# One order for the last four normalisations across three engines, and four gathered rows moved from ahead of the expert loop into it

## The chip, the core and the metric

The kernel runs on one core of a Trainium2 chip. The metric is device microseconds of one execution; the time before is the median of three runs, 1522.99 us (1522.4 to 1523.95). The core's engines are TensorE (PE, matmuls; PEld is its weight load), VectorE (DVE), ScalarE (ACT), GpSimd (POOL) and SyncE (SP, which here issues transfers). Line numbers are those of the kernel before.

## What is computed

One encoder layer on 512 tokens of width 1024: layer norm, a projection, neighbourhood and latent attention, layer norm, then the part that matters here, a feed-forward of 16384 experts (`peer_ffn`), a gated extra term, and a last layer norm:

```python
idx = (e1 * PEER_N_KEYS + e2).reshape(PEER_CHUNK, PEER_HEADS * PEER_TOPK)
g = jax.nn.softmax(cv, axis=-1).reshape(PEER_CHUNK, -1)
u = u_table[idx]
hpre = jnp.einsum('td,ted->te', xb, u)
act = g * jax.nn.gelu(hpre, approximate=False)
return jnp.einsum('te,ted->td', act, v_table[idx])
...
h = layer_norm(DN_ALPHA * h + ffn + ple, ln2_g[i], ln2_b[i])
```

Each token picks 128 experts (8 heads of 16). An expert is one row of U (1024 numbers) and one of V. `layer_norm` subtracts the mean of a token's 1024 values, divides by the root of the variance plus 1e-5, multiplies by `ln2_g` and adds `ln2_b`.

## The kernel before

Tokens lie in four row blocks of 128 partitions, numbered 0 to 3. Block 0 (`c < NGC`) goes the sparse way: for each of its 128 picks k, GpSimd issues an indirect transfer that gathers one U row per token into a `gat` tile (128 x 1024, 512 KB in all; eight such buffers), and DVE multiplies it by the tokens and sums (`gather_u`, L1264, or `rows`, L964, for the first 31). After a Gelu, 128 V rows are gathered in the same way and added, weighted, into `base[0]` (`gather_v`, L1273). Together these are 257 steps (`gather_steps`, L1279).

Blocks 1 to 3 (384 tokens) go the dense way: `lead_block` (L1031) and `expert_in` multiply them by all 128 blocks of U, and the loop at L1340 multiplies the gated result by all 128 blocks of V, in a chosen `order`. Per loop step n it loads one V block (512 KB, `load_v`), splits it into a high and a low part (`split`, L106: ScalarE rounds, DVE subtracts), every second step scales and splits a G tile, and does 18 matmuls of 512 columns into six PSUM accumulators `acc[c][hf]`, two halves for each of the three blocks. The last four steps are held back in `late` and done accumulator by accumulator (L1388), so that `acc` of block 1 is ready first and that of block 3 last.

The gather steps are dealt out along this loop. `room(n)` (L1329) gives each step a weight; after step n, as many gather steps have been issued as the share of weights used up so far (L1384). `PRE` says how many U rows were done ahead of the loop: 31 in an earlier stage (`BESIDE`), `SOME` = 4 whose transfers are issued first in the block at L1307, ahead of the two loads of the first G tile on GpSimd's queue, and six more (`PRE` - `BESIDE` - `SOME`) behind those loads. By this arithmetic 27 gather steps fall to n = 112 to 124. The order on DVE and SP is the program's (`manual_schedule`); in the block at L1307 also that of ScalarE, TensorE and GpSimd.

The end (L1394 to L1406) has no such order: for each block, the two halves of `acc` are added into `base[c]` with a running sum (blocks 1 to 3, L1402), then `layer_norm` (L135). Block 0 takes mean and variance by batch-norm statistics on DVE (L142); the others take the mean from the sums and the variance from a Square on ScalarE (L152). Then a root on ScalarE (L155), a refinement by four 128x1 operations on DVE (`rsqrt_refine`, L128), two 128x1024 operations on DVE (L162 or L164, L165), and one transfer out per block. The four chains are interleaved by the scheduler. GpSimd has no part in it.

Of the kernel before, what the change touches and what calls it, by code (L numbers as in the profile page):

```python
# [9 lines left out]
F32 = mybir.dt.float32  # L10
# [4 lines left out]
AF = mybir.ActivationFunctionType  # L15
OP = mybir.AluOpType
# [3 lines left out]
D = 1024  # L20
# [7 lines left out]
EPS = 1e-5  # L28
# [8 lines left out]
WIDE = 40  # L37
LEAD = 104
# [3 lines left out]
PACE = 1.07  # L42
AHEAD = 14.0
LAG = 6.0
PRE = 41
SOME = 4
EARLY = 15
EARLY_AT = 4
BESIDE = 31
# [12 lines left out]
GATS = 8  # L62
NO_GATHER = 1
GE_AHEAD = 12
CLOSE = 31
# [13 lines left out]
def tile_encoder_layer(ctx: ExitStack, tc: tile.TileContext, A: dict, out: bass.AP):  # L79
    nc = tc.nc  # L80
# [3 lines left out]
    small = ctx.enter_context(tc.tile_pool(name="small", bufs=4))  # L84
# [11 lines left out]
    w_top = keep.tile([128, 2], F32, name="w_top")  # L96
# [533 lines left out]
    for hf in range(2):  # L630
        hs = slice(hf * 512, (hf + 1) * 512)
# [13 lines left out]
    NGC, NDC = N_G // 128, N_D // 128  # L645
# [607 lines left out]
    pG = ctx.enter_context(tc.tile_pool(name="pG", bufs=1, reuse_waits="tile"))  # L1253
    pP = ctx.enter_context(tc.tile_pool(name="pP", bufs=2, reuse_waits="tile"))
    psA = ctx.enter_context(tc.tile_pool(name="psA", bufs=1, space=PSUM, reuse_waits="tile"))
    acc = [[psA.tile([128, 512], F32, name=f"acc{c}{hf}") for hf in range(2)] for c in range(NDC)]
# [16 lines left out]
    def gather_v(c, k):  # L1273
        u = pG.tile([128, D], F32, name="gat", bufs=GATS)
        nc.gpsimd.indirect_dma_start(out=u[:], out_offset=None, in_=v_rows,  # L1275
                                     in_offset=bass.IndirectOffsetOnAxis(ap=i_sel[:, c, k:k + 1], axis=0))
        nc.vector.scalar_tensor_tensor(base[c], u, hdot[:, c, k:k + 1], base[c], op0=OP.mult, op1=OP.add)  # L1277

    def gather_steps():  # L1279
        for c in range(NGC):  # L1280
# [19 lines left out]
    def blocks_ahead(n):  # L1300
        for _ in range(8 * n):
            next(pe_work, None)

    steps = list(gather_steps())
    late = []

    with tc.manual_schedule(engines={nc.vector.engine, nc.scalar.engine, nc.tensor.engine, nc.sync.engine,  # L1307
                                     nc.gpsimd.engine}):
# [13 lines left out]
        for n in range(2):  # L1322
            v_cut[n] = cut_v(n)
            blocks_ahead(1)
        for k in range(BESIDE + SOME, PRE):
            gather_u(0, k)
        for _ in pe_work:
            pass
    def room(n):  # L1329
        if n < NO_GATHER or n > 124:  # L1330
            return 0.0
        return 2.2 if n + LEAD < 126 else 1.6 if n < CLOSE else 1.0 if n < WIDE else 1.42 if n < 112 else 1.9

    rooms = sum(room(n) for n in range(128))
    done, spent = PRE, 0
    with tc.manual_schedule(engines={nc.vector.engine, nc.sync.engine}):
# [56 lines left out]

    lg = row_bcast(pG, A["ln2_g"], "gat", GATS)  # L1394
    lb = row_bcast(pG, A["ln2_b"], "gat", GATS)
    for c in range(4):
        fsum = None
        if c >= NGC:
            fsum = small.tile([128, 2], F32, name="fsum", bufs=2)
            for hf in range(2):  # L1400
                hs = slice(hf * 512, (hf + 1) * 512)
                nc.vector.scalar_tensor_tensor(base[c][:, hs], acc[c - NGC][hf], w_top[:, 0:1] if c == NGC else 1.0,  # L1402
                                               base[c][:, hs], op0=OP.mult, op1=OP.add,
                                               accum_out=fsum[:, hf:hf + 1])
        layer_norm(base[c], lg, lb, fsum, None if fsum is None else pG.tile([128, D], F32, name="gat", bufs=GATS))
        nc.sync.dma_start(out[c * 128:(c + 1) * 128, :], base[c])  # L1406


# [85 lines left out]
```

## Time and profile before

| | |
|---|---|
| median of three runs | 1522.99 us |
| the profiled execution | 1525.05 us |
| its span, first to last instruction | 1523.2 us |
| busy PE / DVE / ACT / POOL | 95% / 83% / 36% / 41% |
| mean granted TensorE clock | 0.99 |
| moved by DMA | 456.15 MB, mean 299 GB/s |
| first matmul of the V loop | 915.1 us from the span's start |
| last subtraction of the loop on DVE ends | about 1501.9 us |
| last matmul begins | 1511.1 us |

Times in a row are microseconds from the span's start and the duration. Behind `x` stands the number of instructions merged into a row; in square brackets, how long the engine sat idle before it and what ended that. `a<-b,c` names the tile written and the tiles read. "issue" is time in which the engine waited for nothing that the profile shows.

### The profile page before, as it was taken

What the parts mean: (1) busy time and instruction counts of PE and PEld (TensorE: products, weight loads), DVE (VectorE), ACT (ScalarE), POOL (GpSimd) and SP (SyncE); (2) the same over time, 40 slices, a digit from 0 to 9 for tenths busy, and PEclk for the clock granted to TensorE, in tenths of its full rate; (3) what the DMA queues carried; (4) which work ended last, traced back from release to release, by engine and by line L of the source; (5) the groups of instructions that cost most, each with busy time, mean ns of one, the idle gap of its engine ahead of it and who ended that gap; (6) DMA issues with size and microseconds to landing.
All of it is one profiled execution on the core that took longest, in us unless ns stands there. A gap on an engine that the chain in (4) does not pass through costs nothing.

```text
span 1523.2 us, 21811 instructions
## 1 busy us (share of the span) xinstructions
PE 1451.8 (95%) x7715; PEld 1221.4 (80%) x7715; DVE 1267.5 (83%) x2638; ACT 544.4 (36%) x893; POOL 627.7 (41%) x537
## 2 busy tenths in 40 slices
PE   6999999999999999898989989999999999999996
PEld 4788777788888888687877868898788888888875
DVE  7376795668999999899779938988789999989998
ACT  3265685333311232222322323444333333333333
POOL 1013110043355644253235345655545555556560
PEclk9999999999999999899999999999999999999999
DMA  7233241194389999899879999999999999999992
GB/s 238 66 115 92 86 125 43 49 300 147 105 291 322 394 416 413 301 396 398 314 258 409 412 388 392 391 392 335 341 389 396 402 398 398 402 396 400 394 362 113
DMA packets 188414, 456.15 MB, mean 299 GB/s; under 512 B 16400, under 2 KB 80272, under 8 KB 185232
## 3 DMA queue, kind: packets, MB, share of 16 engines
q1 hardware_dynamic: 121264, 211.45, 38.8%
q0 software_dynamic: 58400, 208.69, 36.3%
q10 hardware_dynamic: 8640, 34.61, 5.6%
q8 instruction: 61, 1.00, 0.3%
q14 instruction: 49, 0.40, 0.1%
HBM read 413.01 MB, written 38.80 MB: 297 GB/s over the span
## 4 chain that ended last, share of the span: by engine, by line
PE 42%; DVE 20%; issue 15%; DMA 14%; POOL 6%; ACT 2%; SPq 1%; POOLq 0%; DVEq 0%; ACTq 0%
DMA raw<-in_v_rows_dram 7%; PE acc L126 5%; PE acc L124 5%; PE acc L125 5%; PE pj L124 3%; PE pj L125 3%; PE pj L126 3%; DMA raw<-in_uT_dram 3%; DVE base L1277 3%; PE mm L1042 3%; POOL row L968 2%; PE mm L124 2%; PE mm L126 2%; POOL wlo L968 2%; PE mm L125 2%
## 5 line engine op out<-in xcount | busy, mean ns | idle before, releaser
L1275 POOL DMA_INDIRECT gat<-in_v_rows_dram,i_sel x128 | 192.8, 1506 | 140.8 <-DVE base L1277 119.5
L1042 PE MATMUL hp<-whole,raw 128*128 128x256 f32 x816 | 193.4, 393 | 21.1 <-DMA raw<-in_uT_dram 21.1
L1260 POOL DMA_INDIRECT gat<-in_u_rows_dram,i_sel x97 | 149.4, 1541 | 121.8 <-DVE gat L1266 93.6
L1042 PEld LDWEIGHTS hp<-whole,raw 128*128 128x128 f32 x816 | 158.9, 197 | 45.6 <-issue 13.2
L126 PE MATMUL acc<-v_hi,a_lo 128*128 128x512 f32 x456 | 178.4, 392 | 2.6 <-DVE a_lo L110 2.5
L124 PE MATMUL acc<-v_hi,a_hi 128*128 128x512 f32 x456 | 178.3, 391 | 1.5 <-ACT v_hi L109 1.1
L125 PE MATMUL acc<-v_lo,a_hi 128*128 128x512 f32 x456 | 177.8, 390 | 0.8 <-DVE v_lo L110 0.8
L109 ACT CAST whi<-raw 128x1024 fp32r<-128x1024 f32 (+4 forms) x103 | 102.7, 997 | 198.7 <-DMA raw<-in_v_rows_dram 101.4
L1277 DVE SCALAR_TENSOR_TENSOR base<-gat,hdot,base 128x1024 f32<-128x1024 f32 x128 | 165.0, 1289 | 1.8
L110 DVE TENSOR_TENSOR wlo<-raw,whi 128x1024 fp32r<-128x1024 f32 (+4 forms) x103 | 118.6, 1152 | 42.7 <-ACT whi L109 41.8
L109 ACT CAST v_hi<-v_raw 128x1024 fp32r<-128x1024 f32 x76 | 79.9, 1052 | 144.7 <-DMA v_raw<-in_v_rows_dram 66.0
L1042 PE MATMUL mm<-whole,raw 128*128 128x256 f32 x560 | 126.7, 382 | 4.4 <-DMA raw<-in_uT_dram 4.4
L126 PE MATMUL acc<-whi,a_lo 128*128 128x512 f32 x312 | 121.6, 390 | 0.3 <-DVE a_lo L110 0.3
L125 PE MATMUL acc<-wlo,a_hi 128*128 128x512 f32 x312 | 121.5, 390 | 0.2 <-DVE wlo L110 0.2
L110 DVE TENSOR_TENSOR v_lo<-v_raw,v_hi 128x1024 fp32r<-128x1024 f32 x76 | 92.6, 1218 | 34.4 <-ACT v_hi L109 34.1
L124 PE MATMUL acc<-whi,a_hi 128*128 128x512 f32 x312 | 120.9, 389 | 0.0
L1266 DVE SCALAR_TENSOR_TENSOR gat<-gat,h 128x1024 f32<-128x1024 f32 x97 | 115.0, 1219 | 6.7 <-DMA gat<-in_u_rows_dram,i_sel 6.7
L1042 PEld LDWEIGHTS mm<-whole,raw 128*128 128x128 f32 x560 | 104.4, 190 | 18.8 <-DMA raw<-in_uT_dram 3.8
L126 PEld LDWEIGHTS acc<-v_hi,a_lo 128*128 128x128 f32 x456 | 85.6, 188 | 23.6 <-DVE a_lo L110 6.2
L124 PEld LDWEIGHTS acc<-v_hi,a_hi 128*128 128x128 f32 x456 | 85.6, 188 | 20.3 <-ACT a_hi L109 1.7
L125 PEld LDWEIGHTS acc<-v_lo,a_hi 128*128 128x128 f32 x456 | 85.7, 188 | 18.1 <-DVE v_lo L110 1.1
L1023 ACT ACTIVATE ge_ring<-hp 128x256 f32<-128x256 f32 x85 | 32.4, 381 | 146.0 <-PE hp L1042 123.9
(395 smaller groups left out, 3382.7 us busy)
## 6 DMA issues: line engine op xcount, KB each, us to landing
raw<-in_uT_dram SPq DMA_DIRECT2D x110, 512.0 KB
v_raw<-in_v_rows_dram SPq DMA_DIRECT2D x78, 512.0 KB
raw<-in_v_rows_dram SPq DMA_DIRECT2D x50, 512.0 KB
g_dram<-g_st ACTq DMA_DIRECT2D x24, 1024.0 KB
ge_dram<-ge_ring ACTq DMA_DIRECT2D x36, 256.0 KB
g_wide<-g_dram SPq DMA_DIRECT2D x9, 1024.0 KB
raw<-in_w_in_dram SPq DMA_DIRECT2D x17, 512.0 KB
raw<-in_w_q_dram SPq DMA_DIRECT2D x16, 512.0 KB
```

Source lines behind the costliest of these rows:

```text
L109: nc.scalar.copy(hi, src)
L110: nc.vector.tensor_tensor(lo, src, r32(hi), op=OP.subtract)
L124: nc.tensor.matmul(ps, a[0], b[0], start=start, stop=False)
L125: nc.tensor.matmul(ps, a[0], b[1], start=False, stop=False)
L126: nc.tensor.matmul(ps, a[1], b[0], start=False, stop=stop)
L968: nc.gpsimd.indirect_dma_start(out=u[:np], out_offset=None, in_=u_rows, in_offset=bass.IndirectOffsetOnAxis(ap=ix[:np, k:k + 1], axis=0))
L1023: nc.scalar.activation(ge_t[i - i % 2][:, i % 2], ps[:, :N_U], AF.Gelu)
L1042: nc.tensor.matmul(ps[:, :N_U], raw[k], whole[:, k, :], start=(k == 0), stop=(k == 7))
L1260: nc.gpsimd.indirect_dma_start(out=u[:], out_offset=None, in_=u_rows, in_offset=bass.IndirectOffsetOnAxis(ap=i_sel[:, c, k:k + 1], axis=0))
L1266: nc.vector.scalar_tensor_tensor(u, u, 1.0, h[c], op0=OP.mult, op1=OP.mult, accum_out=hdot[:, c, k:k + 1])
L1275: nc.gpsimd.indirect_dma_start(out=u[:], out_offset=None, in_=v_rows, in_offset=bass.IndirectOffsetOnAxis(ap=i_sel[:, c, k:k + 1], axis=0))
L1277: nc.vector.scalar_tensor_tensor(base[c], u, hdot[:, c, k:k + 1], base[c], op0=OP.mult, op1=OP.add)
```

## The change

Two things change. First, `PRE` goes from 41 to 37 and `SOME` from 4 to 0: the four early rows are no longer gathered ahead of the G loads; six rows (31 to 36) stay behind them, and the loop deals out 220 steps instead of 216. The weight of n = 112 to 124 goes from 1.9 to 2.1, by which 30 steps fall there.

Second, the end is written out by hand on DVE, ScalarE, GpSimd and SP. The sum for block 0's mean comes from the last `gather_v` (`accum_out`), in place of the batch-norm statistics, and its variance from a Square on ScalarE like the others'. Blocks 0 and 2 finish "aside": ScalarE applies scale and offset (Identity), GpSimd multiplies by `ln2_g` and adds `ln2_b`, and one transfer goes out. Blocks 1 and 3 finish on DVE: one operation `centre`, then two halves with a transfer each.

```diff
-PRE = 41
-SOME = 4
+PRE = 37
+SOME = 0
...
-        nc.vector.scalar_tensor_tensor(base[c], u, hdot[:, c, k:k + 1], base[c], op0=OP.mult, op1=OP.add)
+        nc.vector.scalar_tensor_tensor(base[c], u, hdot[:, c, k:k + 1], base[c], op0=OP.mult, op1=OP.add,
+                                       **({"accum_out": fsum[c][:, 0:1]} if k == 127 else {}))
...
-        return 2.2 if n + LEAD < 126 else 1.6 if n < CLOSE else 1.0 if n < WIDE else 1.42 if n < 112 else 1.9
+        return 2.2 if n + LEAD < 126 else 1.6 if n < CLOSE else 1.0 if n < WIDE else 1.42 if n < 112 else 2.1
...
+    def take(c, hf):
+        hs = halves[hf]
+        nc.vector.scalar_tensor_tensor(base[c][:, hs], acc[c - NGC][hf], w_top[:, 0:1] if c == NGC else 1.0,
+                                       base[c][:, hs], op0=OP.mult, op1=OP.add, accum_out=fsum[c][:, hf:hf + 1])
+
+    def mean(c):
+        if c < NGC:
+            nc.vector.tensor_scalar(neg[c], fsum[c][:, 0:1], -1.0 / D, None, op0=OP.mult)
+        else:
+            nc.vector.tensor_tensor(neg[c], fsum[c][:, 0:1], fsum[c][:, 1:2], op=OP.add)
+            nc.vector.tensor_scalar(neg[c], neg[c], -1.0 / D, None, op0=OP.mult)
+        nc.scalar.activation(pG.tile([128, D], F32, name="gat", bufs=GATS), base[c], AF.Square, bias=neg[c],
+                             accum_out=ve[c])
+
+    def root(c):
+        nc.vector.tensor_scalar(ve[c], ve[c], 1.0 / D, EPS, op0=OP.mult, op1=OP.add)
+        nc.scalar.sqrt(sd[c], ve[c])
+
+    def refine(c):
+        nc.vector.reciprocal(sd[c], sd[c])
+        rsqrt_refine(inv[c], sd[c], ve[c], off[c])
+
+    def aside(c):
+        nc.vector.tensor_tensor(off[c], neg[c], inv[c], op=OP.mult)
+        nc.scalar.activation(base[c], base[c], AF.Identity, bias=off[c], scale=inv[c])
+        nc.gpsimd.tensor_tensor(base[c], base[c], lg, op=OP.mult)
+        nc.gpsimd.tensor_tensor(base[c], base[c], lb, op=OP.add)
         nc.sync.dma_start(out[c * 128:(c + 1) * 128, :], base[c])
+
+    def centre(c):
+        x = pG.tile([128, D], F32, name="gat", bufs=GATS)
+        nc.vector.scalar_tensor_tensor(x, base[c], neg[c], lg, op0=OP.add, op1=OP.mult)
+        return x
+
+    def finish(c, x, hf):
+        hs = halves[hf]
+        nc.vector.scalar_tensor_tensor(x[:, hs], x[:, hs], inv[c], lb[:, hs], op0=OP.mult, op1=OP.add)
+        nc.sync.dma_start(out[c * 128:(c + 1) * 128, hs], x[:, hs])
```

The order, each line on the engines that it names above: mean(0); take(1, 0), take(1, 1), mean(1); root(0); take(2, 0); refine(0), aside(0); one = centre(1); root(1); take(2, 1), mean(2); refine(1), finish(1, one, 0), finish(1, one, 1); root(2); take(3, 0); refine(2), aside(2); take(3, 1), mean(3); three = centre(3); root(3), refine(3); finish(3, three, 0), finish(3, three, 1).

More of the change, by code (lines that the diff above doesn't have):

```diff
@@ L1305, in tile_encoder_layer @@
     late = []
+    fsum = [small.tile([128, 2], F32, name=n, bufs=4 if n == "ln_mu" else 2)
+            for n in ("ln_mu", "fsum", "fsum", "ln_mu")]
     with tc.manual_schedule(engines={nc.vector.engine, nc.scalar.engine, nc.tensor.engine, nc.sync.engine,
@@ L1395, in tile_encoder_layer @@
     lb = row_bcast(pG, A["ln2_b"], "gat", GATS)
[L1396 to L1405, printed above, removed]
-        nc.sync.dma_start(out[c * 128:(c + 1) * 128, :], base[c])
+    neg = [small.tile([128, 1], F32, name="ln_y0") for c in range(4)]
@@ new lines, in tile_encoder_layer @@
+    ve = [small.tile([128, 1], F32, name="ln_ve") for c in range(4)]
+    sd = [small.tile([128, 1], F32, name="ln_sd") for c in range(4)]
+    inv = [small.tile([128, 1], F32, name="ln_y") for c in range(4)]
+    off = [small.tile([128, 1], F32, name="ln_t") for c in range(4)]
+    halves = [slice(0, 512), slice(512, 1024)]
+    def take(c, hf):
+        hs = halves[hf]
+        nc.vector.scalar_tensor_tensor(base[c][:, hs], acc[c - NGC][hf], w_top[:, 0:1] if c == NGC else 1.0,
+                                       base[c][:, hs], op0=OP.mult, op1=OP.add, accum_out=fsum[c][:, hf:hf + 1])
@@ new lines, in finish @@
+    def finish(c, x, hf):
+        hs = halves[hf]
+        nc.vector.scalar_tensor_tensor(x[:, hs], x[:, hs], inv[c], lb[:, hs], op0=OP.mult, op1=OP.add)
+        nc.sync.dma_start(out[c * 128:(c + 1) * 128, hs], x[:, hs])
+    with tc.manual_schedule(engines={nc.vector.engine, nc.scalar.engine, nc.gpsimd.engine, nc.sync.engine}):
+        mean(0)
+        take(1, 0)
+        take(1, 1)
+        mean(1)
+        root(0)
+        take(2, 0)
+        refine(0)
+        aside(0)
+        one = centre(1)
+        root(1)
+        take(2, 1)
+        mean(2)
+        refine(1)
+        finish(1, one, 0)
+        finish(1, one, 1)
+        root(2)
+        take(3, 0)
+        refine(2)
+        aside(2)
+        take(3, 1)
+        mean(3)
+        three = centre(3)
+        root(3)
+        refine(3)
+        finish(3, three, 0)
+        finish(3, three, 1)
```

## The prediction

> **What bounds the kernel now.** The profiled execution spans 1523.2 us and took 1525.05 us, so 1.85 us lie around the span; the median of the runs is 1522.99 us. I make the sum against the span and add it to the median. A measurement of this kernel can tell about 0.2% (3 us) from no change.
>
> I read the page first, then a table by stage around the two edited places (the columns are the window, its length, busy us and count of PE, PEld, DVE, ACT and POOL, the granted clock, the DMA share and GB/s).
>
> ```profile
> PE 1451.8 (95%) x7715; PEld 1221.4 (80%) x7715; DVE 1267.5 (83%) x2638; ACT 544.4 (36%) x893; POOL 627.7 (41%) x537
> ```
>
> ```profile
> 880.00:892.00 12.00, 5.07 (x23) 3.80 (x21) 5.12 (x10) 0.77 (x2) 1.89 (x3) 0.97 1.02 368
> 892.00:896.00 4.00, 3.43 (x8) 2.81 (x9) 0.00 (x0) 0.00 (x0) 3.08 (x4) 0.50 1.03 374
> 896.00:900.00 4.00, 4.00 (x15) 3.28 (x15) 0.00 (x0) 0.38 (x1) 3.09 (x4) 0.72 1.02 367
> ...
> 1100.00:1440.00 340.00, 339.36 (x1495) 280.13 (x1494) 309.13 (x316) 119.23 (x125) 190.48 (x125) 1.00 1.04 397
> 1440.00:1492.00 52.00, 50.49 (x218) 40.08 (x217) 51.54 (x48) 15.68 (x17) 28.27 (x19) 1.00 0.92 353
> ```
>
> The whole says PE; the stages say three different things. From 1100 to 1440 PE is the limit (busy 339.36 of 340.00) while DVE has 31 us to spare: a gather row added there is hidden. From 1440 to 1492, the blocks 112 to 123, DVE has half a microsecond left in 52: a row added there is paid. From 880 to 900, just ahead of the loop, PE is busy 5.07 of 12 us and the DMA share is above 1: DMA is the limit. After 1502 come the four normalisations, where the wait that ends last must be followed op by op.
>
> **The opening: four rows fewer.** Timelines of PE, POOL, DVE and ACT, and the DMA total from 865 to 905.5:
>
> ```profile
> 882.40 3.72 PE L1042 MATMUL hp<-whole,raw 128*128 128x256 f32 x16 [1.06 <-DMA raw<-in_uT_dram]
> 892.57 6.49 PE L1042 MATMUL hp<-whole,raw 128*128 128x256 f32 x16 [6.44 <-DMA raw<-in_uT_dram]
> 898.90 7.07 PE L1042 MATMUL hp<-whole,whi 128*128 128x256 f32 x32
> ```
>
> ```profile
> 865.08 1.43 POOL L1260 DMA_INDIRECT gat<-in_u_rows_dram,i_sel  x1 [0.30 <-issue]
> ...
> 878.53 0.94 POOL L1260 DMA_INDIRECT gat<-in_u_rows_dram,i_sel  x1 [0.30 <-DMA raw<-in_uT_dram]
> ```
>
> ```profile
> 890.56 1.23 DVE L1266 SCALAR_TENSOR_TENSOR gat<-gat,h 128x1024 f32<-128x1024 f32 x1 [1.34 <-DMA gat<-in_u_rows_dram,i_sel]
> ...
> 904.36 1.23 DVE L110 TENSOR_TENSOR v_lo<-v_raw,v_hi 128x1024 fp32r<-128x1024 f32 x1 [12.56 <-ACT v_hi L109]
> ```
>
> ```profile
> 905.47 1.04 ACT L109 CAST whi<-raw 128x1024 fp32r<-128x1024 f32 x1 [1.14 <-DMA raw<-in_uT_dram]
> ```
>
> ```profile
> DMA packets 3921, 15.87 MB, mean 392 GB/s; under 512 B 416, under 2 KB 416, under 8 KB 3555
> ```
>
> The four SOME rows go out on POOL from 865.08 to 878.53, ahead of both loads of the first G tile; DVE consumes the last one at 890.56 and then sits idle for 12.56 us. So their DVE work (4 x 1.23 us) is hidden and its removal worth nothing, and so is the POOL time; the cover is that idle stretch. What they cost is traffic: 4 x 128 rows x 4 KB = 2.10 MB, at 392 GB/s 5.35 us, in a stretch where PE waits 6.44 us for a U block and ScalarE waits for the next (905.47). With PRE at 37 the same six rows (31 to 36 instead of 35 to 40) stay behind the G loads, and eight gat buffers cap what is drawn forward, so the bytes are really gone from this stage. The first G load moves ahead on POOL's queue from behind 878.53 to 865 at the earliest; its bytes were due in this stage anyway. Bounds: nothing, if the queues re-divide the time and the U block still lands last; and PE's whole stall, 6.44 us of idle plus the slow matmuls behind it: at 0.22 us each (7.07 us for 32) 34 would fit between 892.57 and 900, and at the clock of 0.50 and 0.72 there were 23, so 2.4 us more, together 8.8. I take the bytes, 5.35, because ScalarE's wait for DMA at 905.47 caps what PE could win alone.
>
> Of the four rows one returns in blocks 0 to 111 (the count that `room` gives falls from 4 behind to 3 there) and three in blocks 112 to 124 (27 before, 30 after: 1.9 becomes 2.1). The first is hidden under PE unless DMA, at 397 GB/s beside it, is as tight as PE, when it costs 0.52 MB / 392 GB/s = 1.35; I take half. Gain up to block 112: 5.35 - 0.65 = 4.7 us.
>
> **The tail: three rows more.** From the chain of waits, two pairs of rows between their neighbours, and the group of blocks 112 to 123:
>
> ```profile
> 1440.41 1.21 DVE base L1277
> ...
> 1442.84 0.15 DVE wlo L110
> ...
> 1443.98 1.33 DVE base L1277
> ...
> 1446.69 0.44 issue
> ```
>
> ```profile
> L1277 DVE SCALAR_TENSOR_TENSOR base<-gat,hdot,base 128x1024 f32<-128x1024 f32 x25 | 32.3, 1291 | 0.5
> ```
>
> Two rows take 2.43 us and two take 2.71, so 1.29 each, as the group's mean. DVE is full here, and everything behind stands in its order: 3 x 1.29 = +3.9 us. It could be as little as 2.5 if DVE enters block 112 further ahead.
>
> **The end.** Before, the last subtraction of the loop ends at 1501.9 and the span ends 21.3 us later. Rows of DVE, ACT and SP:
>
> ```profile
> 1500.78 1.22 DVE L110 TENSOR_TENSOR v_lo<-v_raw,v_hi 128x1024 fp32r<-128x1024 f32 x1
> ...
> 1503.11 0.74 DVE L1402 SCALAR_TENSOR_TENSOR h<-acc,w_top,h 128x512 f32<-128x512 f32 x1
> ...
> 1517.71 0.16 DVE L131 TENSOR_TENSOR ln_t<-ln_t,ln_y 128x1 f32<-128x1 f32 x1
> 1517.91 0.15 DVE L132 TENSOR_SCALAR ln_t<-ln_t 128x1 f32<-128x1 f32 x1
> ...
> 1518.29 1.28 DVE L165 SCALAR_TENSOR_TENSOR h<-h,ln_y,gat 128x1024 f32<-128x1024 f32 x1
> ```
>
> ```profile
> 1499.80 1.28 ACT L155 ACT_TABLE_LOAD   x1
> ...
> 1506.70 1.15 ACT L152 ACTIVATE gat<-h,ln_mu 128x1024 f32<-128x1024 f32 x1 [1.80 <-DVE ln_mu L149]
> ```
>
> The earlier normalisation has ScalarE's order Square, then root, as the new end has:
>
> ```profile
> 278.80 1.15 ACT L152 ACTIVATE raw<-h,ln_mu 128x1024 f32<-128x1024 f32 x1 [5.90 <-DVE ln_mu L149]
> ...
> 280.06 1.28 ACT L155 ACT_TABLE_LOAD   x1
> 281.35 0.20 ACT L155 ACTIVATE ln_sd<-ln_ve 128x1 f32<-128x1 f32 x1
> ```
>
> There the table load comes only behind the Square. Now it is hidden at 1499.80, because the root is first; afterwards it stands behind two Squares and ahead of root 0, on the path. The Trainium skill, in "ScalarE: Activation LUTs", section What ACT_TABLE_LOAD costs, gives about 2.66 us for a switch, load and drain; here the root follows 1.29 us after the load's start, so I go by the row, and by the page the end would be 1.4 us later (1531.6).
>
> GpSimd gets four operations, multiply and add for row blocks 0 and 2. What it does to DVE is shown where GpSimd computes earlier (POOL rows, DVE rows, POOL's group):
>
> ```profile
> 369.50 2.47 POOL L852 TENSOR_TENSOR wlo<-raw,whi 128x1024 fp32r<-128x1024 f32 x1 [4.10 <-ACT whi L851]
> 382.88 2.58 POOL L852 TENSOR_TENSOR wlo<-raw,whi 128x1024 fp32r<-128x1024 f32 x1 [4.51 <-ACT whi L851]
> ```
>
> ```profile
> 369.84 2.26 DVE L740 TENSOR_TENSOR cand<-v_all 128x32 f32<-128x32 f32 x2
> ...
> 383.14 0.21 DVE L801 TENSOR_REDUCE gs<-gws 128x4 f32<-128x64 f32 x1
> 383.27 2.34 DVE L784 TENSOR_TENSOR prod<-prod 128x256 f16<-128x256 f16 x1
> ...
> 393.55 0.28 DVE L784 TENSOR_TENSOR prod<-prod 128x256 f16<-128x256 f16 x1
> ```
>
> ```profile
> L852 POOL TENSOR_TENSOR wlo<-raw,whi 128x1024 fp32r<-128x1024 f32 x14 | 33.7, 2407 | 52.9 <-ACT whi L851 52.9
> ```
>
> An operation of 0.28 us takes 2.34 and ends 0.1 us after GpSimd's; so does the tiny one at 369.84. The reduction, with one tensor read, passes. So a DVE operation that reads two SBUF tensors stands still until GpSimd's ends, and in `refine` and `mean` even 128x1 operations are of that kind. `take` reads PSUM and one SBUF tensor; I let it pass.
>
> Now in the times of the old trace, durations from the rows (small dependent operation 0.2, as from 1517.71 to 1517.91). The first half of `take(1)` is ready at 1503.1; two halves to 1504.6; `mean(1)` 1504.95; Square 1 (1.15 + 0.1 of its read) 1506.2; table load 1507.5; root 1507.7. DVE waits there, and with it all that is queued behind `refine(0)`. `refine(0)` and the offset, six small steps, 1508.85. Identity 0 on ScalarE (a Square's time) 1510.1, `centre(1)` beside it. GpSimd multiplies to 1512.5; `mean(2)` stands still until then. Its add runs to 1515.0; `refine(1)` stands still until then, ends 1515.8, `finish(1)` (two halves of 1.28) 1517.1; root 2 1517.6 with `take(3, 0)` beside it; `refine(2)` and offset 1518.95; Identity 2 1520.2, with `take(3, 1)` and `mean(3)` beside it. `centre(3)` holds the multiply of block 2 until 1521.3; it ends 1523.7, its add 1526.2, and `refine(3)` is caught behind one or both; then 0.8 and 1.25 us to 1528.2. SP's queue has block 2's output ahead of the last halves, but that is ready at 1526.2 and delays nothing. The sum that block 0's mean now takes from its last gather row is one more small read on DVE, under 0.1 us. Before, 3.6 us lay between DVE's last operation (1518.29 + 1.28) and the end of the span, for 512 KB; I take 3.0 for the last 256 KB: 1531.2, 8.0 us later than 1523.2. Bounds: +5 (DVE wins every turn against the second add), +9.5.
>
> Sum: -4.7 + 3.9 + 8.0 = +7.2 us: 1530.2.
>
> **The rivals.** *GpSimd runs beside DVE* (not slower): the operations of the end, mostly f32 and 1024 wide or one element wide, interleave where the f16 ones above did not. Then `mean(2)` is done at 1511.1, `refine(1)` at 1512.0, `finish(1)` 1513.3, offset 2 at 1515.2, Identity 2 1516.5, GpSimd 1518.9 and 1521.3, and block 2's output lands 3.6 us later, 1525.0: the end costs +1.8, the sum is +1.0: 1524.0. It decides if DVE loses under 3 us in all to GpSimd. For it: the reduction that passes. Against: 369.84 is f32 and tiny. The Trainium skill, in "SBUF — State Buffer", section SBUF: two separate sides, has the port pair of the two engines as an exclusive lock for a whole instruction, against DVE operations with two SBUF inputs; by that rule this rival is out, and the trace agrees (2.34 for 0.28). I leave it 17%.
>
> *The opening gives PE's whole stall*: -8.8 + 0.65 + 3.9 + 8.0 = +3.8: 1526.8. For it: the clock falls to 0.50 only because of the long wait. Against: the wait at 905.47. 10%.
>
> *The opening gives nothing* because the queues re-divide: +3.9 + 8.0 = +11.9: 1534.9. For it: POOL's queue draws six rows forward. 7%.
>
> *Both good cases together*: -8.15 + 3.9 + 1.8 = -2.5, 1520.5, and faster by over 0.2% if DVE also enters the tail ahead. 10%.
>
> **How the numbers follow.** My forecast has 56%, with its own range 1527 to 1533 (opening 3 to 6.5, tail 2.5 to 4.2, end +5 to +9.5). Slower by over 0.2% (above 1526.0): 54 of the 56, 6 of the 10, the 7 and 2 of the 17, so 69%. Within 0.2%: 2 of the 56, 4 of the 10, 11 of the 17, 4 of the last 10, so 21%. Faster (below 1519.9): 4 of the 17 and 6 of the last 10, 10%. The range reaches down into the second case and up toward the fourth, 1522.8 to 1534.4; it leaves out the last 10, about half of the 7 and a few of the 17.
>
> **What would show it.** PE's wait near 892 shrinks from 6.44 to under 2 us and the granted clock there is near 1; blocks 112 to 124 last 3.9 us longer; a table load stands behind two Squares; DVE's `mean(2)` and `refine(1)` show 128x1 operations of one to two us that end with GpSimd's; from DVE's last subtraction to the end of the span some 29 us instead of 21.3. If those small operations last 0.2 us each, the forecast's largest term is wrong, and if PE still waits 6 us near 892 the first is.

## The result: 14 us slower, nearly twice what was forecast

After the change the median is 1537.7 us (1535.04 to 1540.15, six runs), beside 1524.1 us for the kernel before on the same chip (1522.4 to 1526.57, six runs): a ratio of 1.0088, 95% interval 1.0073 to 1.0103, or +13.6 us by the medians and 11 to 16 by the interval. The direction was forecast (slower, 69%); the time lies above the range, which ended at 1534.4. Executions of one and the same program differ by some us here (the kernel before gave 1520.1 to 1529.0 in 23 later runs), so the two profiled executions, 1523.2 and 1533.8 us of span, lie 10.6 apart and not 13.6; places are compared below by the lengths of stages in several traces, times by medians.

The page and the table by stage of the kernel after; the windows are those shown of before, with one more just ahead of the loop:

```profile
PE 1453.1 (95%) x7715; PEld 1223.0 (80%) x7715; DVE 1271.6 (83%) x2637; ACT 548.0 (36%) x897; POOL 627.2 (41%) x541
```

```profile
880.00:892.00 12.00, 10.07 (x38) 8.26 (x39) 0.00 (x0) 0.94 (x3) 2.36 (x3) 0.86 1.01 408
892.00:896.00 4.00, 4.00 (x20) 3.54 (x19) 0.04 (x1) 1.45 (x3) 3.09 (x4) 1.00 1.03 358
896.00:900.00 4.00, 4.00 (x21) 3.51 (x20) 2.97 (x3) 2.89 (x4) 3.08 (x4) 1.00 1.03 408
...
908.00:914.00 6.00, 4.46 (x23) 4.42 (x24) 4.18 (x6) 0.94 (x2) 2.48 (x2) 0.72 1.03 408
1100.00:1440.00 340.00, 338.47 (x1489) 278.80 (x1488) 308.10 (x317) 118.45 (x125) 185.43 (x126) 1.00 1.04 397
1440.00:1492.00 52.00, 47.52 (x196) 37.33 (x195) 51.46 (x47) 14.38 (x15) 31.72 (x22) 0.97 0.95 361
```

The first rows are what I forecast: from 880 to 892 PE is busy 10.07 us instead of 5.07, and from 892 to 900 it is full at a granted clock of 1.00, where it had 0.50 and 0.72. But from 908 to 914 PE has a hole of 1.5 us and a clock of 0.72. In the tail DVE is full as before (51.46 of 52) and PE gets less done (47.52 instead of 50.49).

**The opening.** PE ahead of the loop; the last row is the first matmul of the loop (915.1 before, 913.8 now):

```profile
881.78 9.28 PE L1042 MATMUL hp<-whole,raw 128*128 128x256 f32 x32 [2.03 <-DMA raw<-in_uT_dram]
...
905.58 0.39 PE L124 MATMUL hp<-hTh,whi 128*128 128x256 f32 x1 [1.06 <-ACT ge_ring L1023]
...
909.54 0.39 PE L126 MATMUL hp<-hTh,wlo 128*128 128x256 f32 x1 [3.46 <-DVE wlo L110]
...
913.77 0.40 PE L124 MATMUL acc<-v_hi,a_hi 128*128 128x512 f32 x1
```

The wait of 6.44 us for a U block is gone; all that PE waits for U blocks here is the 2.03 us at 881.78, where it was 7.5 us in two waits. Then PE stops again, for 3.46 us, now for DVE's `wlo`, the low part of the next U block. DVE in the kernel after:

```profile
899.35 1.22 DVE L110 TENSOR_TENSOR v_lo<-v_raw,v_hi 128x1024 fp32r<-128x1024 f32 x1 [1.03 <-ACT v_hi L109]
900.49 1.22 DVE L1266 SCALAR_TENSOR_TENSOR gat<-gat,h 128x1024 f32<-128x1024 f32 x1
...
905.78 1.23 DVE L1266 SCALAR_TENSOR_TENSOR gat<-gat,h 128x1024 f32<-128x1024 f32 x1 [0.53 <-DMA gat<-in_u_rows_dram,i_sel]
...
908.27 1.22 DVE L110 TENSOR_TENSOR wlo<-raw,whi 128x1024 fp32r<-128x1024 f32 x1
```

and in the kernel before:

```profile
908.90 1.22 DVE L1266 SCALAR_TENSOR_TENSOR gat<-gat,h 128x1024 f32<-128x1024 f32 x1
...
910.04 1.22 DVE L110 TENSOR_TENSOR wlo<-raw,whi 128x1024 fp32r<-128x1024 f32 x1
```

All six held rows (31 to 36) now stand in a row between the second `v_lo` and that `wlo`, 7.8 us from 900.49 to 908.27; before, one row stood there and the others came behind. What `wlo` is made from had long been there: ScalarE, in the kernel after, was done with `whi` by 900.3.

```profile
899.22 1.05 ACT L109 CAST whi<-raw 128x1024 fp32r<-128x1024 f32 x1
```

Neither constant names this order. In the program's text the six rows stand ahead of that `wlo` in both kernels; the scheduler merges the stretch ahead of the loop with the loop's beginning, and with the new `PRE` and `SOME` the merge came out otherwise. Why it did is not shown.

**The tail.** From the start of the G scaling of step 112 to that of step 124, before and after:

```profile
1437.73:1491.91 54.18, 52.67 (x227) 41.91 (x226) 53.72 (x50) 16.99 (x19) 29.43 (x20) 1.00 0.93 355
```

```profile
1435.39:1493.69 58.30, 53.82 (x224) 42.49 (x224) 57.69 (x54) 16.50 (x18) 33.33 (x23) 0.97 0.94 357
```

It is 4.12 us longer, 3.97 of it busy time of DVE.

**The end.** DVE's rows from the last subtraction on, then ScalarE, GpSimd and SyncE:

```profile
1504.12 0.15 DVE L1413 TENSOR_SCALAR ln_y<-ln_mu 128x1 f32<-128x1 f32 x1
1505.84 0.75 DVE L1408 SCALAR_TENSOR_TENSOR h<-acc,w_top,h 128x512 f32<-128x512 f32 x1 [1.58 <-PE acc L126]
...
1510.48 0.16 DVE L1425 RECIPROCAL ln_sd<-ln_sd 128x1 f32<-128x1 f32 x1 [2.16 <-ACT ln_sd L1422]
...
1513.52 1.88 DVE L1415 TENSOR_TENSOR ln_y<-fsum 128x1 f32<-128x1 f32 x1
...
1515.69 2.13 DVE L130 TENSOR_TENSOR ln_t<-ln_ve,ln_sd 128x1 f32<-128x1 f32 x1
...
1524.67 1.41 DVE L130 TENSOR_TENSOR ln_t<-ln_ve,ln_sd 128x1 f32<-128x1 f32 x1
...
1526.50 2.00 DVE L133 TENSOR_TENSOR ln_y<-ln_t,ln_sd 128x1 f32<-128x1 f32 x1
1528.53 1.41 DVE L1443 SCALAR_TENSOR_TENSOR gat<-gat,ln_y 128x512 f32<-128x512 f32 x2
```

```profile
1507.69 1.15 ACT L1417 ACTIVATE gat<-h,ln_y 128x1024 f32<-128x1024 f32 x1 [2.16 <-DVE ln_y L1416]
...
1508.95 1.28 ACT L1422 ACT_TABLE_LOAD   x1
1510.25 0.20 ACT L1422 ACTIVATE ln_sd<-ln_ve 128x1 f32<-128x1 f32 x1
```

```profile
1513.04 2.34 POOL L1432 TENSOR_TENSOR base<-base,gat 128x1024 f32<-128x1024 f32 x1 [28.68 <-ACT base L1431]
1515.46 2.35 POOL L1433 TENSOR_TENSOR base<-base,gat 128x1024 f32<-128x1024 f32 x1
1522.96 3.10 POOL L1432 TENSOR_TENSOR h<-h,gat 128x1024 f32<-128x1024 f32 x1 [5.16 <-ACT h L1431]
1526.14 2.34 POOL L1433 TENSOR_TENSOR h<-h,gat 128x1024 f32<-128x1024 f32 x1
```

```profile
1528.50 0.33 SPq L1434 DMA_DIRECT2D out_dram<-h  x1
1529.31 0.99 SPq L1444 DMA_DIRECT2D out_dram<-gat  x2
```

The four 128x1 operations of 1.41 to 2.13 us end within 0.1 us of the four GpSimd operations; left alone they last 0.16. That is 6.8 us of standstill. The table load stands behind the Square of block 1, and DVE waits 2.16 us for the root behind it. From the last subtraction's end (1504.1, where the next row begins) to the end of the span are 29.7 us, beside 21.3. (The table below takes the row's start plus its duration for that end, which is 0.1 us later.)

The same marks in the traces of all kernels that were run (the columns: first matmul of the loop; start of the G scaling of steps 112 and 124; end of the last subtraction, its row's start plus duration; span; and what lies between these two):

```
                           first acc    112      124    last sub.   span    end
before                        915.1   1437.7   1491.9   1502.0   1523.2   21.2
1 new end alone               913.1   1433.8   1488.0   1498.1   1527.2   29.1
2 rows alone                  915.0   1435.9   1494.2   1504.8   1526.8   22.0
after                         913.8   1435.4   1493.7   1504.2   1533.8   29.6
3 one-tensor small steps      914.3   1436.9   1496.0   1506.3   1534.7   28.4
4 rows spread                 909.8   1433.1   1491.4   1501.5   1530.5   29.0
5 without GpSimd              918.3   1443.1   1501.4   1511.7   1538.9   27.2
6 early table                 915.9   1439.0   1497.3   1507.4   1536.0   28.6
7 before, lighter tail        915.7   1444.3   1495.8   1507.9   1531.3   23.4
8 old rows, end on DVE        911.7   1437.0   1491.2   1501.7   1522.3   20.6
9 rows spread, old end        906.7   1427.7   1486.0   1496.1   1518.6   22.5
10 rows spread, end on DVE    909.3   1430.9   1489.2   1499.3   1520.5   21.2
11 GpSimd for block 0 alone   914.1   1436.1   1494.4   1504.5   1532.1   27.6
12 as 10, weight 1.9          909.5   1433.0   1488.2   1498.3   1518.9   20.6
```

### The profile page after: what moved, and what is told of

Its sections match the earlier page's. It is cut to its first block, busy times and chain, and to the rows that moved or that the text cites. A ratio compares the mean times of both kernels' runs of the same rounds, so it can differ in the third digit from the quotient of the medians.

```text
span 1533.8 us, 21829 instructions
## 1 busy us (share of the span) xinstructions
PE 1453.1 (95%) x7715; PEld 1223.0 (80%) x7715; DVE 1271.6 (83%) x2637; ACT 548.0 (36%) x897; POOL 627.2 (41%) x541
## 4 chain that ended last, share of the span: by engine, by line
PE 44%; issue 17%; DVE 16%; DMA 11%; POOL 8%; ACT 2%; SPq 1%; POOLq 0%; DVEq 0%; ACTq 0%
PE acc L124 7%; PE acc L126 7%; PE acc L125 7%; DMA raw<-in_v_rows_dram 5%; PE pj L124 3%; PE pj L125 3%; PE pj L126 3%; POOL row L968 3%; POOL whi L968 3%; POOL wlo L968 3%; DVE base L1277 2%; PE mm L124 2%; DMA v_raw<-in_v_rows_dram 2%; PE mm L126 2%; PE mm L125 2%
## 5 line engine op out<-in xcount | busy, mean ns | idle before, releaser
L1275 POOL DMA_INDIRECT gat<-in_v_rows_dram,i_sel x128 | 189.5, 1480 | 141.4 <-DVE base L1277 120.6
L1042 PE MATMUL hp<-whole,raw 128*128 128x256 f32 x816 | 191.6, 390 | 15.2 <-DMA raw<-in_uT_dram 15.1
L1042 PEld LDWEIGHTS hp<-whole,raw 128*128 128x128 f32 x816 | 157.6, 196 | 39.2 <-issue 12.5
L1042 PE MATMUL mm<-whole,raw 128*128 128x256 f32 x560 | 127.1, 382 | 5.5 <-DMA raw<-in_uT_dram 5.5
L1042 PEld LDWEIGHTS mm<-whole,raw 128*128 128x128 f32 x560 | 104.3, 190 | 20.3 <-DMA raw<-in_uT_dram 3.8
L125 PEld LDWEIGHTS acc<-v_lo,a_hi 128*128 128x128 f32 x456 | 86.1, 189 | 18.3 <-DVE v_lo L110 1.1
```

Source lines behind the costliest of these rows:

```text
L125: nc.tensor.matmul(ps, a[0], b[1], start=False, stop=False)
L1042: nc.tensor.matmul(ps[:, :N_U], raw[k], whole[:, k, :], start=(k == 0), stop=(k == 7))
```

## The experiments

My theory after the result had two parts: the end costs its 8 us for the forecast reasons, GpSimd's turns above all; and the opening loses its gain because six rows stand ahead of `wlo`. The rivals: the rows cost what they cost in the tail, whatever the opening does; and the end is long for its order and its waits, not for GpSimd.

### 1 and 2: each half alone

```diff
-PRE = 37
-SOME = 0
+PRE = 41
+SOME = 4
...
-        return 2.2 if n + LEAD < 126 else 1.6 if n < CLOSE else 1.0 if n < WIDE else 1.42 if n < 112 else 2.1
+        return 2.2 if n + LEAD < 126 else 1.6 if n < CLOSE else 1.0 if n < WIDE else 1.42 if n < 112 else 1.9
```

This is experiment 1 against the kernel after; experiment 2 is the kernel before with the same three lines the other way.

> The new end alone, with the four early rows and the weights of before. Theory A (the end costs about 8.4 us, the rows about 2.2): 8 to 9 us slower than before, a span near 1531.5, and the loop's last subtraction on DVE ends where it did, near 1502. Rival B (the two parts work on each other, and the 3 us by which the medians stand further apart than the two profiled executions belong to the end): 11 us or more.

> The moved rows alone, with the end of before. Theory A: about 2 us slower than before; the first matmul into acc near 913.8 instead of 915.1, blocks 112 to 123 about 58.3 us instead of 54.2. Rival B: the rest of the medians' difference sits here, 4 to 6 us slower. Rival C (my prediction's sums for opening and tail): 0.8 us faster.

Measured, beside a median of 1524.5 before: the end alone 1532.07 (ratio 1.0057, 1.0041 to 1.0074), the rows alone 1531.04 (1.0049, 1.0032 to 1.0066). So +7.6 and +6.5, together 14.1: the halves add up to the whole, 13.6. By the marks the end alone lengthens the last stretch by 7.9 us (29.1 against 21.2). The rows alone: blocks 112 to 124 by 4.1, the way from there to the last subtraction by 0.5, the end by 0.8, and the opening gives nothing. The forecast had -0.8 for this half, and here is the miss; 6.5 is also nearer the rival's 4 to 6 than the 2 of my theory.

### 4 and 9: the six rows out of `wlo`'s way

```diff
-        for k in range(BESIDE + SOME, PRE):
-            gather_u(0, k)
+        held_rows = [(k, fetch_u(0, k)) for k in range(BESIDE + SOME, PRE)]
...
+            for k, u in held_rows[2 * n:2 * n + 2]:
+                gather_u(0, k, u)
             spent += room(n)
```

Experiment 4 is the kernel after with this; experiment 9 is the same with the end of the kernel before. The transfers stay where they were.

> The changed kernel, with the six rows 31 to 36 fetched at the same place but multiplied in the loop's first three steps, two in each, in place of six in a row ahead of the loop. Theory A (six multiplications in a row on DVE stand in front of the low part of the second U block, and PE waits for that 3.5 us and runs slow behind it): the first matmul into acc comes at 907 to 909 in place of 913.8, and the time falls by 4 to 6 us. Rival (the opening is bound by DMA, and the U block or the G tile is not there earlier): it stays within 1 us of 913.8.

> The kernel before, its own end kept, with the change's row counts and weight (37 rows ahead of the blocks, none tied into the first blocks, weight 2.1) and the six held rows multiplied two each in the loop's first three steps instead of six in a row ahead of them. Theory (the rows lose because six multiplications stand in a row before the second U block's low part; without that the opening gives its 4 to 5 us and the tail's three rows take 4.1 back): TensorE's first acc matmul at 909 to 911.5, blocks 112 to 124 in 58.3 us, the time within 1.5 us of the kernel before and 5 to 7 below the run that moved the rows alone. Rival (the loop's tail with 30 rows is dear in itself, whatever the opening does, because the later start of the rows' reads is given back by the DMA engines): 1529 to 1532, like the rows alone.

Experiment 4: 1532.07 us, +7.6 over its runs of before (1.0049, 1.0032 to 1.0065) where the kernel after has +13.6, and the same as the new end alone. Experiment 9: 1523.55 beside 1523.66 before (0.9991, 0.998 to 1.0003), where the rows alone have +6.5. In experiment 4 PE, a line of the list of waits from 880 to 915 (us in total, times, longest), and DVE:

```profile
890.11 3.72 PE L1042 MATMUL hp<-whole,raw 128*128 128x256 f32 x16 [2.09 <-DMA raw<-in_uT_dram]
...
909.78 0.40 PE L124 MATMUL acc<-v_hi,a_hi 128*128 128x512 f32 x1
```

```profile
PE hp L1042 <- DMA raw<-in_uT_dram: 3.9, 2, 2.1
```

```profile
904.29 1.23 DVE L110 TENSOR_TENSOR wlo<-raw,whi 128x1024 fp32r<-128x1024 f32 x1 [0.94 <-PE hp L1042]
...
909.25 1.22 DVE L1266 SCALAR_TENSOR_TENSOR gat<-gat,h 128x1024 f32<-128x1024 f32 x1
```

The wait for `wlo` is gone: DVE makes it at 904.29, though the U blocks came 2 to 3 us later than in the kernel after (PE starts `hp<-whole,whi` at 893.67 instead of 890.89). The loop starts at 909.8, 906.7, 909.3 and 909.5 in the four traces with spread rows, 908.8 on average; at 913.9 in the four with the old rows (915.1, 913.1, 915.7, 911.7), and at 915.2 in the six that have all six in a row. So four rows fewer give 5.1 us, for the 5.35 of the prediction, and the order on DVE takes 6.4 away. The traces already differ by 3 us at 728 us (the first `mm` matmul of L1042), ahead of everything that the change touches; counted from there the three means are 181.1, 186.4 and 188.0 us: 5.4 given and 7.0 taken away. The rival falls with experiment 9: the tail is 58.3 us long there too, and the time is that of before. The two are equal because rows moved from the opening to the tail are paid at both places: 5.1 gained on average, 4.1 lost in the tail and, in experiment 9, 1.3 lost in the end (22.5 for 21.2).

### 3, 5 and 11: how GpSimd's turns cost

Experiment 3 changes the 128x1 steps so that none reads two tensors: the second becomes a scalar per partition. Like this, for all of `mean`, `refine` and the offset:

```diff
-            nc.vector.tensor_tensor(neg[c], fsum[c][:, 0:1], fsum[c][:, 1:2], op=OP.add)
-            nc.vector.tensor_scalar(neg[c], neg[c], -1.0 / D, None, op0=OP.mult)
+            nc.vector.tensor_scalar(neg[c], fsum[c][:, 0:1], fsum[c][:, 1:2], -1.0 / D, op0=OP.add, op1=OP.mult)
```

> The changed kernel, with the 128x1 operations of mean, refine and the offset written with one tensor and a per-partition scalar in place of two tensors; the same values, three operations in place of four in refine's product and one in place of two in mean. Blocking theory (a DVE operation with two SBUF tensors stands still while GpSimd computes): the operations of 1.4 to 2.1 us fall to 0.2, and the end gets 3 to 5 us shorter, part of it lost again where the halves of finish meet GpSimd's add. Rival (the end is a chain of latencies, and GpSimd's share in the stalls is a coincidence of waits): only the operations that are gone count, 0.6 to 1 us.

1536.7 us, +12.2 over before (1.008, 1.0063 to 1.0097): 1.4 less than the kernel after has, which these intervals cannot tell from nothing, and where I had expected the end 3 to 5 shorter. In the end DVE's longest rows and one of its small steps, and GpSimd's rows:

```profile
1515.48 0.22 DVE L1425 TENSOR_SCALAR ln_t<-ln_ve,ln_sd 128x1 f32<-128x1 f32 x1
...
1516.42 3.91 DVE L1445 SCALAR_TENSOR_TENSOR gat<-gat,ln_y 128x512 f32<-128x512 f32 x2
...
1526.32 3.61 DVE L1445 SCALAR_TENSOR_TENSOR gat<-gat,ln_y 128x512 f32<-128x512 f32 x2
```

```profile
1514.69 2.35 POOL L1434 TENSOR_TENSOR base<-base,gat 128x1024 f32<-128x1024 f32 x1 [28.08 <-ACT base L1433]
1517.12 2.67 POOL L1435 TENSOR_TENSOR base<-base,gat 128x1024 f32<-128x1024 f32 x1
...
1526.71 2.67 POOL L1435 TENSOR_TENSOR h<-h,gat 128x1024 f32<-128x1024 f32 x1
```

The small steps now pass at 0.2 us beside GpSimd. But what they had waited for, the next large operation meets instead: the pair of `finish` takes 3.91 and 3.61 in place of 1.41, 4.7 us of standstill for 6.8. Part of these 2.1 us is lost again behind DVE: from its last row to the end of the span are 4.8 us, beside 3.9.

Experiment 5 takes GpSimd out: blocks 0 and 2 end on DVE like 1 and 3.

```diff
-        aside(0)
+        zero = centre(0)
+        finish(0, zero, 0)
+        finish(0, zero, 1)
...
-        aside(2)
+        two = centre(2)
+        finish(2, two, 0)
+        finish(2, two, 1)
```

In experiment 11 only block 2 is taken back (the lower half of the diff). In both the Square writes its unused result to a tile of another pool.

> The kernel after, with the two normalisations that ScalarE and GpSimd shared (chunks 0 and 2) finished on DVE like chunks 1 and 3: centre, then two finish halves; no GpSimd work in the end. Theory (GpSimd's four turns, 2.34 to 2.4 us each and 9.7 in all, stand in DVE's path): they go, and DVE gets two centres of 1.28 and four halves of 0.7 to 0.75, about 5.5. The time falls by 4 to 5 us to 1532 to 1534; from DVE's last subtraction to the end 24.5 to 26 us instead of 29.7; no 128x1 operation over 0.3 us. Rival (GpSimd's turns lie beside DVE's work, and the end is long for its order, its table load and its waits for ScalarE): the 5.5 us come on top, the time is 1541 to 1544.

> The kernel after with GpSimd keeping chunk 0 alone (two turns of 2.35 us instead of four); chunk 2 is finished on DVE by a centre and two halves. Theory (each GpSimd turn holds up DVE by about 1.75 us, 7.0 in all in the kernel after, and a chunk done on DVE costs 1.28 and 1.41, so that each chunk taken back from GpSimd saves about 3.5 less 2.7, and a last store of the same size): the stretch from the last subtraction to the end is 28.3 to 29 us, between the 29.7 of the kernel after and the 27.2 without GpSimd; the time 0 to 2 below the kernel after. Rival (the first turn alone makes the delay, since it meets the mean and the refinement at the narrowest place): 29.7 or more, no gain.

Experiment 5: 1539.72 us, +15.1 (1.0098, 1.0073 to 1.0122), no gain on the kernel after, where I had expected 4 to 5. Experiment 11: 1534.86, +11.2 (1.0069, 1.0053 to 1.0084), 2.4 less than the kernel after has. By place both shorten the end, to 27.2 and 27.6 us from 29.6, the second by more than the 0.7 to 1.4 expected. In experiment 5:

```profile
1513.51 0.75 DVE L1408 SCALAR_TENSOR_TENSOR h<-acc,w_top,h 128x512 f32<-128x512 f32 x1 [1.76 <-PE acc L126]
...
1518.15 0.16 DVE L1425 RECIPROCAL ln_sd<-ln_sd 128x1 f32<-128x1 f32 x1 [2.16 <-ACT ln_sd L1422]
```

No 128x1 operation is over 0.3 us any more. 6.8 us of standstill go and two centres of 1.28 and two pairs of 1.41 come, 5.4 us: that leaves 1.4, and the last store, which no longer has another block's 512 KB just ahead of it on SP, is 0.6 shorter (3.3 against 3.9 us behind DVE's last row); together 2.0 of the 2.4. I had counted all 9.7 us of GpSimd's turns as standstill; 6.8 was it. So GpSimd's help takes more of DVE's time than it saves, but little more. The wait for PE's first sum, 1.58 us in the kernel after, is anything from 0.9 to 2.0 in the traces with its end or a variant of it (0.91 in experiment 11), so ends that lie within 1 us of each other are not told apart.

The rival is right about the larger part: without GpSimd the end is still 6.0 us longer than before, and between the last subtraction and its own last row DVE is idle for 5.2 us, beside 0.3 before. The two waits shown are 3.9 of these. In the end of experiment 8, below, DVE is idle for 0.2. So of the 8.4 us that the new end adds, about 2.4 go with GpSimd and 6.0 stay with the order as written and its waits.

Why experiment 5's total did not fall is open: its loop ended 7.5 us later than in the kernel after, 4.5 of it by the loop's first matmul and 2.1 already at 728 us, ahead of everything that the change touches, though the order of every engine up to the last subtraction is the same; its four runs are 1539.5 to 1540.6. I have no experiment on that.

### 6: the root's table ahead of the Squares

```diff
+        nc.vector.tensor_scalar(off[3], fsum[0][:, 0:1], 0.0, 1.0, op0=OP.mult, op1=OP.add)
+        nc.scalar.sqrt(sd[3], off[3])
         mean(0)
```

> The kernel after with one small root of a number that is thrown away ahead of the first Square, so that ScalarE loads the root's table there, while DVE still works on blocks; the two Squares and the root behind it are as they were. Theory (the table load of 1.28 us stands in DVE's wait of 2.16 us for the first root): DVE waits 0.9 us or less, the span's last part is 28.4 us instead of 29.7, the time 1536.4 or 1.3 less than the kernel after. Rival (behind the root DVE meets GpSimd at the same spot later anyway, or the load now delays the first Square): no change, within 0.4 us.

1537.55 us (1.0079, 1.0054 to 1.0104): by the time no difference that can be told. By place the theory holds. ScalarE and DVE:

```profile
1505.17 1.28 ACT L1448 ACT_TABLE_LOAD   x1
1507.46 0.20 ACT L1448 ACTIVATE ln_sd<-ln_t 128x1 f32<-128x1 f32 x1 [1.01 <-DVE ln_t L1447]
1507.57 1.14 ACT L1417 ACTIVATE gat<-base,ln_y 128x1024 f32<-128x1024 f32 x1
```

```profile
1512.67 0.16 DVE L1425 RECIPROCAL ln_sd<-ln_sd 128x1 f32<-128x1 f32 x1 [0.74 <-ACT ln_sd L1422]
```

The load is done at 1506.45, before the loop's last subtraction ends (1507.36), DVE's wait for the first root is 0.74 instead of 2.16, the end 28.6 instead of 29.6. The Squares behind the root's table need no load of their own.

### 7: fewer rows in the old tail

```diff
-        return 2.2 if n + LEAD < 126 else 1.6 if n < CLOSE else 1.0 if n < WIDE else 1.42 if n < 112 else 1.9
+        return 2.2 if n + LEAD < 126 else 1.6 if n < CLOSE else 1.0 if n < WIDE else 1.42 if n < 112 else 1.7
```

> The kernel before with one number changed, the weight of blocks 112 to 124 from 1.9 to 1.7: 24 rows there instead of 27, and 3 more in blocks 40 to 111. Theory (in the last 13 blocks each row costs DVE its whole 1.29 us, in blocks 40 to 111 a row costs 0 to 1.35, half of that as the prediction took it): blocks 112 to 124 are 3.9 us shorter and the blocks before them up to 2 us longer, the time 1520.2 to 1522.6, about 2 to 4 below the kernel before. Rival (in blocks 40 to 111 each row costs the 1.32 us that its 0.52 MB take on the DMA engines): within 0.5 us of the kernel before.

1528.8 us (1.0027, 1.0013 to 1.004): 4.2 slower, which neither side expected. Blocks 112 to 124 are shorter, 51.5 us for 54.2, but then PE stops for the last `whi`. PE, ScalarE, and that `whi` in the kernel before:

```profile
1502.94 0.88 PE L124 MATMUL acc<-whi,a_hi 128*128 128x512 f32 x2 [3.01 <-ACT whi L109]
```

```profile
1500.90 1.04 ACT L109 CAST v_hi<-v_raw 128x1024 fp32r<-128x1024 f32 x1 [3.53 <-DMA v_raw<-in_v_rows_dram]
1501.85 1.04 ACT L109 CAST whi<-v_raw 128x1024 fp32r<-128x1024 f32 x1
1502.91 1.28 ACT L155 ACT_TABLE_LOAD   x1
```

```profile
1494.01 1.05 ACT L109 CAST whi<-v_raw 128x1024 fp32r<-128x1024 f32 x1 [0.49 <-PE acc L126]
```

ScalarE now makes the last `whi` behind the `v_hi` of the last V block, which waits for its transfer until 1500.90; in the kernel before it stood ahead of that one. The old end, which has no order of its own, has also moved block 0's normalisation in among the last blocks, on DVE from 1499.68 to 1502.59 and on ScalarE from 1502.91. Why one weight changes these orders is not shown. The 2.7 us that the tail saved were lost there (12.1 us for 10.1 from step 124 to the last subtraction, and 23.4 for 21.2 in the end), and the blocks before 112 took 528.6 us (three more rows) beside 520.7, 522.6 and 525.3 in the three other traces with the old rows. This split is rough: the profiled execution, 1533.0 us, is 4 above its kernel's median.

### 8, 10 and 12: an end on DVE alone, and where the rows should go

The last three runs use an end of my own: no GpSimd, the table loaded early as in 6, the small steps as in 3, and the four chains interleaved by hand, so that each Square and root has another block's work beside it; the Square writes to the other pool as in 5. Its beginning:

```diff
+        mean(0)
+        x[0] = centre(0)
+        root(0)
+        take(1, 0)
+        refine(0, 0)
+        take(1, 1)
+        refine(0, 1)
+        mean(1)
+        refine(0, 2)
+        x[1] = centre(1)
```

Experiment 8 has the old rows, 10 the spread rows of experiment 4, and 12 those with the weight of the tail back at 1.9 (27 rows there instead of 30, 115 instead of 113 in blocks 40 to 111, one more in 22 to 39).

> The loop of the kernel before (rows and weights as they were) with an end of my own, all on DVE: chunk 0's sum from its last row and its squares from ScalarE, so that the 1.28 us of statistics go; the root's table loaded ahead of the first Square; the 128x1 steps in forms with one tensor; the last finish in halves, so that 256 KB go out last in place of 512 KB. Theory: DVE's part of the end, 17.7 us packed in the kernel before, loses 1.6 us of statistics and about 0.8 of small steps, and the last store about 0.5: from the last subtraction to the end 18.3 to 19.7 us instead of 21.3, the time 1521.5 to 1523 (1.5 to 3 below the kernel before). Rival (the order written out makes DVE wait for ScalarE's Squares and roots, 2.6 us from one to the next chunk, where the scheduler's interleaving hid them): 21 to 24 us, no gain or up to 3 us slower.

> The rows of the run before this one (37, spread over the first steps, weight 2.1) with the end of my own that is all on DVE. Theory: the two parts add up as they did in the first four runs; the end is 20.6 us from the last subtraction as in the run with the old rows (21.2 to 22 in kernels with the old end), so the time is 0.5 to 1.5 below the rows with the old end, 1521.5 to 1524. Rival (with 30 rows in the tail TensorE ends late against DVE, and DVE waits for the sums 1.6 us as in the kernel after): 1.5 us more, 1524 to 1526.

> The run with the spread rows and the end of my own, with the tail's weight back at 1.9: 27 rows in blocks 112 to 124 instead of 30, and three more in blocks 22 to 111. Theory (in the tail a row costs DVE 1.29 us, and in blocks 22 to 111, where the DMA engines are at 0.99 to 1.01 of their time, its 0.52 MB cost 1.3 us too): within 1 us of the run with weight 2.1, 1521.5 to 1524. Rival (in those blocks a row is hidden): 3 to 4 us below it, 1518 to 1520, and the best kernel of all.

Experiment 8: 1522.95 beside 1524.61 (0.9987, 0.9972 to 1.0001), at the edge of what can be told; its end is 20.6 us, not the 18.3 to 19.7 expected. DVE's part is 17.5 us (1501.57 to 1519.03), no shorter than the 17.7 of before: the last block's steps stand alone, and `finish` in halves costs 1.41 for 1.28. Experiment 10: 1523.13 (0.9995, 0.9985 to 1.0004), as the theory had it, and no gain.

Experiment 12: 1520.37 beside 1523.66 (0.9975, 0.9964 to 0.9986), 3.3 us faster than the kernel before and 17 faster than the kernel after. It is the only run that is clearly faster than the kernel before, and my theory of it (within 1 us of experiment 10) fell; it is 2.8 us faster than that, a little short of the rival's 3 to 4. Three rows taken from the tail shorten it by 3.1 us (55.2 for 58.3) and lengthen the way from the loop's start to step 112 by 1.9 (523.5 for 521.6), 0.6 each; the end is 0.6 shorter. That way varies by 4 us between traces with equal rows (520.9 to 524.8), so the medians bear more: three rows at 4.1 us in the tail are worth 2.8 less in the middle, which leaves them 0.4 each there. By the scatter of the twelve runs of each the 2.8 could be 1.1 to 4.5, and so the 0.4 anything from 0 to 1. In experiment 12 PE has no hole left in the opening:

```profile
900.00:908.00 8.00, 8.00 (x55) 7.54 (x54) 5.00 (x6) 4.74 (x7) 5.13 (x4) 1.00 1.03 409
```

## Why the prediction was too low

**The opening (-4.7): wrong, and the step that failed.** Its bytes were right: PE's waits for U blocks fell from 7.5 to 2.03 us, the clock near 892 rose to 1.00, and with the rows out of the way (4, 9, 10, 12) the loop starts 5.1 us earlier, for 5.35 forecast. What failed is the step from the bytes to the start of the loop. The sum carries the 5.35 us over whole and puts DVE's part in this stretch at nothing ("their DVE work (4 x 1.23 us) is hidden and its removal worth nothing"), on the strength of DVE's idle 12.56 us. That held for the four rows that went. The forecast did not ask it of the six that stay, nor what PE waits for next once the U block comes earlier. It waits for `wlo`, 3.46 us, behind six rows that take 7.8 us on DVE, and the loop starts at 915.2 on average instead of 913.9: +1.3 in place of -5.35. The forecast's own rival "the opening gives nothing" had nearly the size (+11.9), with 7%, but by luck, since its reason was wrong: the queues did not divide the time anew, the bytes were gained.

**One row back at half of 1.35: not contradicted.** Experiment 12 gives 0.4 to 0.6 for such a row, but cannot tell that from 0 or from 1.

**The tail (+3.9): right.** 4.1 in eight traces with 30 rows (58.28 to 58.30), 4.8 in one. Behind it the stretch to the last subtraction grew by 0.4 in the kernel after and 0.5 with the rows alone, which had no term; but it is 10.1 us, as before, in five other traces with 30 rows, so it does not come from the three rows.

**The end (+8.0): right in size,** 7.9 by the end alone, 8.4 in the kernel after. Its times from the last subtraction (1501.9 in the forecast, 1504.1 in the trace), forecast and read: root 0 done 5.8 and 6.3; GpSimd's first turn done 10.6 and 11.3; `finish(1)` 15.2 and 15.7; GpSimd's last turn 24.3 and 24.4; DVE's last operation 26.3 and 25.8; end 29.3 and 29.7. The forecast gave 6.2 of its 8.0 to DVE standing still behind GpSimd (8.0 less the 1.8 of the rival), and 6.8 were measured; but experiment 5 shows that most of that comes back as work on DVE when GpSimd is left out. Two pieces were missed, each under 1 us: `take(1)` began 1.7 us behind the last subtraction and not 1.2, since DVE waited for PE's first sum; and the output of block 2, of which I said that it "delays nothing", was issued at 1528.50, just ahead of the first half, so that 1 MB went out at once and the last store took 3.9 us, not 3.0.

**Two small misreadings.** The 5.07 us of PE are those of 880 to 892, not of 880 to 900, and the two halves of `finish` take 1.41 us together, not 1.28. Neither moves a term by more than 0.3 us.

**Rules weighed.** For the table load the row decides: 1.30 us from its start to the root's (1508.95 to 1510.25), and experiment 6 took 1.42 off DVE's wait at that place. The 2.66 us that the Trainium skill gives in "ScalarE: Activation LUTs", section What ACT_TABLE_LOAD costs, are not seen here. The standstill behind GpSimd is what the Trainium skill calls an exclusive lock in "SBUF — State Buffer", section SBUF: two separate sides, and the traces agree: 0.16 us became 2.13, and in experiment 3, without a second tensor, it stayed near 0.2. The rival in which GpSimd runs beside DVE is out.

The sum by measured terms for the kernel after: opening +1.3 (915.2 for 913.9), one row 0.5, tail +4.1, behind it +0.4, end +8.4: +14.7, within the interval of 11 to 16. The opening and its one row make +1.8 of it where -4.7 was forecast: 6.5 us, about what the forecast missed (7.2 for 13.6).

## What to carry to other kernels

When a stall on one engine goes, list what its next instructions wait for on every other engine, and how many microseconds of work stand ahead of that there: the gain is what is left after the second-latest. Here that was `wlo`, behind six rows on DVE. Where two hand-ordered stretches are merged, a count changed in one of them can reorder the other, so compare the engine's order and not the constants. An engine that shares something with the critical one helps only if its work is longer than the standstill it makes: here 6.8 us of standstill for 5.4 us of work; and a piece of work that can be dealt out belongs where its engine has time to spare: about 0.5 us a row in the middle of the loop (0 to 1 by the scatter) against 1.3 to 1.4 at either end. And an order written by hand is not better for being written: the same work on DVE alone took 27.2 us in one order (experiment 5) and 20.6 in another (experiment 8, which also loads the table early).

## What the runs showed of the hardware

- A DVE operation on 128x1 that reads two SBUF tensors stands still until the GpSimd operation beside it ends: 1.41 to 2.13 us in place of 0.16. With one tensor and a scalar per partition it takes 0.2 us there, and a large operation is then held instead (3.91 us for 1.41).
- It works the other way too: GpSimd's multiply at 1522.96 took 3.10 us instead of 2.34, beside `centre(3)` on DVE (1522.58, 1.28 us).
- After PE's wait of 3.46 us the matmuls came 0.21 us apart instead of 0.12 for about 3.5 us, and the granted clock from 908 to 914 was 0.72: here the wait cost more than its length.
